# Products of the first two expert units issued unit by unit inside the router stage, and the last token tile scaled and shifted by VectorE

## The chip, the cores and the metric

The kernel runs on one core of a Trainium2 chip. Its time is the device time of one execution in microseconds (us), and the lower of two is the better. Besides TensorE (PE in the rows, its weight loads PEld), VectorE (DVE), ScalarE (ACT), GpSimd (POOL) and SyncE's queue (SP, which issues most transfers) the core has 16 DMA engines, which move data between the device's memory (HBM), SBUF and back.

## The reference, cut to what matters

The model has two layers. Each layer mixes 512 tokens of width 1024 with four branches, normalizes them (layer norm 1, with a gain and a bias), and sends every token to 2 of 32 experts of a hierarchical mixture of experts:

```python
x = _layernorm(alpha * x + mix, ln1_g[l], ln1_b[l])
...
grp_p, grp_idx = lax.top_k(grp_prob, 1)
...
top_p, top_i = lax.top_k(jax.nn.softmax(in_grp, axis=-1), TOP_K)
...
hid = jax.nn.silu(xe @ w_gate[e]) * (xe @ w_up[e])
return hid @ w_down[e]
...
x = _layernorm(alpha * x + ffn, ln2_g[l], ln2_b[l])
```

All matrices are float32. The three matrices of the 32 experts are 3 MB for each expert, some 100 MB in a layer, and every expert's weights are read once in each layer.

## The kernel before, in words

**Stages.** A layer is the mixer (four branches, gates, output projection), then the router stage at the end of the function `mixer`, then the experts in `moe`, then `combine`. The code from the router stage to the experts stands under a manual schedule: every engine gets its instructions in the order in which they are written.

**Router stage.** The four tiles `r[0]` to `r[3]` hold 128 tokens x 1024 each. For each tile the stage adds the residual, takes the statistics, transposes the tile, multiplies it with the router's matrix, and chooses two experts for each token (`R.choose`: maxima, and comparisons whose results are `oo` and `lt`, then `ob`). Tiles 0 to 2 are chosen together, tile 3 later. `R.count` and `R.totals` count with small products how many tokens went to each expert before this one. `R.slots` works out from the counts which token goes to which of 1024 slots; its result `toki` starts the gathers, which fetch the rows of the tokens from `x1_dram`. `R.plan` gives on VectorE the order of the experts by load and writes it into registers that SP reads for the addresses of expert weights.

**Tile 3.** Tiles 0 to 2 are multiplied with the gain (`lng`) and shifted by the bias (`lnb`) on GpSimd in `affine` (L994, L995) and written to `x1_dram` from GpSimd's queue. Tile 3 is scaled on ScalarE (`raw_affine`) and then goes through the same `affine`.

**Units.** Experts 0 to 3 (`LEAD`) are taken in fixed pairs: unit 0 is experts 0 and 1, unit 1 is experts 2 and 3. Their tokens are not gathered: `one_hot(t)` makes a matrix `lone` of 0 and 1 (128 tokens x 4 experts x 64 places), and `lead(t)` multiplies it with `r[t]`. In the kernel before, `lead` takes the four experts in one product of 256 columns, summed over the four tiles in four PSUM banks. In `moe`, `lead_window(u)` copies a unit's columns to SBUF (`xw`), and `gemm(u, c)`, for c from 0 to 3, multiplies them with gate and up weights (L1457; I call these gate products). `hidden(u)`, `hidden_t(u)` and `down(u)` follow with the activation, a transpose and the products with the down weights (L1495). `R.left_over()` and `R.rows()` work out where results are written: a chain between TensorE (L1319 to L1322), VectorE (L1325 to L1358) and TensorE again (L1360). `turned(j)` transposes the j-th gathered tile into `xs` (L1539), from which all later units take their tokens (`window`).

**Weights.** All expert weights pass through `est`, a stream of 1 MB buffers in a ring: 7 `er0`, 2 `raw`, 2 `er2`, then 2 `er1`. I number the transfers of a layer. Transfers 1 to 8 are the gate and up weights of units 0 and 1, 9 to 12 their down weights. Transfer 13 is the first whose address comes from a register. Transfers 14 to 21 go into the buffers of 1 to 8, so each waits until the gate products that read this buffer are done, and 22 goes into the buffer of transfer 9, which `down(0)` reads. All of them are issued in order from SP's queue. The limit on their number is 11 within the router stage, and 22 until the last `turned`:

```python
est.limit = 2 * (ER + MR) + ER_M + ER2
...
turned(7)
ring.cycle += [(R.ep, "er2")] * 2
est.bufs += 2
est.limit = 1 << 30
```

Of the kernel before, what the change touches and what calls it, by code (L numbers as in the profile page):

```python
# [10 lines left out]
F32 = mybir.dt.float32  # L11
# [13 lines left out]
D = 1024  # L25
# [79 lines left out]
def mixer_moe_kernel(ctx: ExitStack, tc: tile.TileContext, a, out, dbg=None):  # L105
# [63 lines left out]
    def ps_mm():  # L169
        return pbank("mm", 3)  # L170

    def ps_s():
        return pbank("s", 2)
# [10 lines left out]
    class Ring:  # L184
# [5 lines left out]
        def more(self, pl, tag, n):  # L190
            self.cycle += [(pl, tag)] * n
            self.bufs[tag] = self.bufs.get(tag, 0) + n
# [126 lines left out]
    def mixer(l, wpool_, wts, raws, xpool, xh, xl, par, ready):  # L319
# [716 lines left out]
        def raw_affine(t):  # L1036
            m = mv[t]
            act(r[t], r[t], AF.Identity, scale=m[:, 2:3], bias=m[:, 3:4])
            affine(t)

        def one_hot(t):

            m = small.tile([128, LEAD, 1], F32, name="lm", bufs=2)
            DVE.scalar_tensor_tensor(m[:, :, 0], R.rank(t), 1.0, R.ob[:, 0, t, :LEAD], op0=OP.add, op1=OP.mult)
            ones[t] = R.ep.tile([128, LEAD, HALF], F32, name="lone", bufs=2)
# [3 lines left out]
        def lead(t, k0=0, k1=KD):  # L1049
            if t + k0 == 0:  # L1050
                R.lead.extend((ps_s(), ps_s(), ps_mm(), ps_mm()))
            for k in range(k0, k1):
                PE.matmul(R.lead[k // 2][:, k % 2 * 256:k % 2 * 256 + 256], r[t][:, k * 128:(k + 1) * 128],
                          ones[t].rearrange("p e j -> p (e j)"), start=t + k % 2 == 0, stop=t == 3, skip_group_check=True)

        ones = {}
# [45 lines left out]
        est = Stream(ep, "er", ER + MR + ER_M + ER2 + 1, 2048)  # L1102
# [19 lines left out]
        raw_affine(3)  # L1122
# [7 lines left out]
        lead(0, 0, 4)  # L1130
# [16 lines left out]
        return R, toki, manual, epool, ring, est, gs  # L1147
# [4 lines left out]
    class routing:  # L1152
# [60 lines left out]
        def slots(self, rp, scratch, beside):  # L1213
# [26 lines left out]
            rone = self.ep.tile([128, 2, 4, 128], BF, name="rone", bufs=1)  # L1240
            pt_ = ps_y()
            for q in range(2):
                for t in range(4):
                    DVE.tensor_scalar(rone[:, q, t], io, low[:, q, t:t + 1], 0.0, op0=OP.add, op1=OP.is_equal)
                    for w in range(2):
                        PE.matmul(pt_[:, :8], rone[:, q, t], hval[:, q, t, w], start=q + t + w == 0,
                                  stop=q + t + w == 5)
# [82 lines left out]
        def rows(self):  # L1330
# [24 lines left out]
            one = T("rone2", [8, 128], BF)  # L1355
            p = ps_t()
            for j in range(8):
                DVE.tensor_scalar(one[:, j], bfc[:, 4], low[:, j:j + 1], 0.0, op0=OP.add, op1=OP.is_equal)  # L1358
                for w in range(2):
                    PE.matmul(p[:, :n], one[:, j], hv[:, w, j], start=j + w == 0, stop=j + w == 8)  # L1360
# [20 lines left out]
    def moe(l, R, toki, manual, epool, ring, est, gs):  # L1381
# [4 lines left out]
        ring.more(er2, "er1", ER2)  # L1386
# [3 lines left out]
        st = {}  # L1390
# [40 lines left out]

        def lead_window(u):
            xw = xa.tile([128, KD, CAP], F32, name="xw", tag="xw", bufs=2)
            for b, p in enumerate(R.lead):
                (DVE.tensor_copy if b % 2 else ACT.copy)(xw[:, 2 * b:2 * b + 2], p.rearrange("p (k n) -> p k n", k=2)[
                    :, :, u * CAP:(u + 1) * CAP])
            st[u] = dict(X=xw)
# [105 lines left out]

        est.limit = 2 * (ER + MR) + ER_M + ER2
        est.bufs = ER + MR + ER_M + ER2 - 1
# [21 lines left out]
        gemm(1, 2)  # L1567
        gemm(1, 3)
# [259 lines left out]
```

## Time and profile before

| what | value |
|---|---|
| time, median of 3 runs | 1587.07 us (1584.9 to 1587.2) |
| the profiled execution | 1588.08 us, of which the span from the first to the last instruction is 1586.3 us |
| busy: PE, DVE, ACT, POOL | 92%, 45%, 36%, 9% of the span |
| granted TensorE clock, mean over the span | 0.972 of full speed |
| transfers | 324.59 MB, mean 205 GB/s |

The profile is of one execution. Times in it count from the start of the span. A granted clock of 1.00 is 2.4 GHz, 0.50 is 1.2 GHz. A row of busy time gives the stretch, its length, the busy time (and instructions) of PE, PEld, DVE, ACT and POOL, then the granted clock, the mean busy share of the DMA engines, and GB/s. A row of a timeline gives start, length, engine, line, what is written and read, shapes and count; the trace counts two instructions for each float32 product, so that x16 in the program's order below is x32 there. The mixer of layer 0 ends at about 493 us, its router stage at about 523 us, its experts at about 760 us; layer 1 has the same stages 787.7 us later, from about 1281 us on.

### The profile page before, as it was taken

The page shows a single profiled execution, that of the slowest core. Times are in us where ns is not written, and L with a number is a line of the kernel's source. Part 1 is how long each engine was busy: PE and PEld are TensorE (multiplying, and loading weights), DVE is VectorE, ACT ScalarE, POOL GpSimd, SP SyncE. Part 2 cuts the span into 40 slices and gives each one's busy share as a digit, 9 for nine tenths or more (in the row PEclk, how much of TensorE's full clock was granted, in tenths as well). Part 3 has the DMA queues.
Part 4 walks back from the last instruction along what each step waited for, and adds up shares of the span by engine and source line. Part 5 has one row for each costly group of instructions (what it writes and reads, how often), then busy time and mean ns, then how long its engine had stood idle before and what let it go on. Part 6 is the DMA issues. An engine that isn't in the chain of part 4 may idle for free. (4 is left out here: it accounts for less than half of the span.)

```text
span 1586.3 us, 17845 instructions
## 1 busy us (share of the span) xinstructions
PE 1463.2 (92%) x6552; PEld 936.0 (59%) x6552; DVE 720.3 (45%) x1382; ACT 564.4 (36%) x1001; POOL 142.8 (9%) x121
## 2 busy tenths in 40 slices
PE   7999999999998999988299999999999989999980
PEld 6766787788887533322197666767888864333320
DVE  7558875434456411110365578864444554111005
ACT  6666435333323211111256654353333223111113
POOL 0000000121006100000000000001210151000000
PEclk9999999999998999999699999999999989999995
DMA  5111122122247999999621121211132579999994
GB/s 212 69 67 67 54 93 83 50 100 93 95 193 293 366 406 423 422 421 418 274 87 54 54 100 54 99 68 67 67 121 86 230 282 381 407 423 421 421 397 169
DMA packets 54042, 324.59 MB, mean 205 GB/s; under 512 B 8640, under 2 KB 9280, under 8 KB 21952
## 3 DMA queue, kind: packets, MB, share of 16 engines
q1 hardware_dynamic: 44880, 299.54, 47.7%
q0 software_dynamic: 9072, 23.89, 4.0%
q8 instruction: 52, 0.85, 0.2%
q14 instruction: 38, 0.31, 0.1%
HBM read 306.62 MB, written 27.26 MB: 210 GB/s over the span
## 5 line engine op out<-in xcount | busy, mean ns | idle before, releaser
L149 PE MATMUL ps_mm<-xh,wh 128*128 128x512 f32 (+1 forms) x768 | 309.1, 403 | 8.7 <-ACT xh L128 8.1
L150 PE MATMUL ps_mm<-xl,wh 128*128 128x512 f32 (+1 forms) x768 | 303.4, 395 | 0.0
L151 PE MATMUL ps_mm<-xh,wl 128*128 128x512 f32 (+1 forms) x768 | 302.4, 394 | 0.0
L1457 PE MATMUL ps_mm<-er,xw 128*64 128x512 f32 (+1 forms) x1024 | 284.9, 598 | 11.2 <-DMA er<-in_w_gu_dram 7.9
L162 DVE TENSOR_TENSOR wl<-raw,wh 128x1280 fp32r<-128x1280 f32 (+2 forms) x116 | 169.7, 1468 | 146.1 <-ACT wh L128 145.8
L1457 PEld LDWEIGHTS ps_mm<-er,xw 128*64 128x64 f32 (+1 forms) x1024 | 88.7, 143 | 175.4 <-issue 143.3
L128 ACT ACTIVATE wh<-raw 128x1280 fp32r<-128x1280 f32 (+2 forms) x116 | 135.2, 1169 | 140.0 <-PE ps_mm L150 99.9
L149 PEld LDWEIGHTS ps_mm<-xh,wh 128*128 128x128 f32 (+1 forms) x768 | 144.1, 188 | 50.6 <-issue 10.1
L151 PEld LDWEIGHTS ps_mm<-xh,wl 128*128 128x128 f32 (+1 forms) x768 | 143.8, 187 | 34.0 <-issue 3.1
L1495 PE MATMUL ps_s<-er,ht 128*64 128x512 f32 (+1 forms) x512 | 147.1, 612 | 17.7 <-DMA er<-in_w_dn_dram 10.7
L150 PEld LDWEIGHTS ps_mm<-xl,wh 128*128 128x128 f32 (+1 forms) x768 | 144.2, 188 | 31.3 <-issue 2.0
L1465 DVE TENSOR_TENSOR sg<-sg,ps_mm 128x256 f32<-128x256 f32 x36 | 15.1, 420 | 253.2 <-ACT sg L128 253.2
L1495 PEld LDWEIGHTS ps_s<-er,ht 128*64 128x64 f32 (+1 forms) x512 | 44.8, 146 | 109.8 <-issue 79.0
L418 POOL TENSOR_TENSOR macc<-macc,sg 128x512 f32<-128x512 f32 x32 | 43.0, 1344 | 697.5 <-PE ps_mm L150 498.9
L128 ACT ACTIVATE sg<-ps_mm,par 128x512 f32<-128x512 f32 x64 | 44.1, 689 | 139.0 <-PE ps_mm L151 139.0
L708 DVE SCALAR_TENSOR_TENSOR cacc<-cvh,par,cacc 128x512 f32<-128x512 f32 x120 | 89.6, 747 | 1.7
L1479 DVE COPY ob<-ps_s 128x512 f32<-128x512 f32 x36 | 24.9, 692 | 132.9 <-PE ps_s L1495 132.9
L417 DVE SCALAR_TENSOR_TENSOR sg<-sg,ps_p 128x512 f32<-128x512 f32 x48 | 33.0, 688 | 105.3 <-PE ps_p L151 97.9
L1484 POOL DMA_INDIRECT ys_dram<-ob,rowi x36 | 35.2, 978 | 407.1 <-DVE xw L1445 301.8
L128 ACT ACTIVATE ht<-ps_t 128x256 f32<-128x256 f32 x36 | 13.8, 383 | 158.3 <-PE ps_t L1472 158.3
L128 ACT ACTIVATE sg<-ps_mm 128x256 f32<-128x256 f32 x36 | 13.8, 383 | 134.7 <-PE ps_mm L1457 134.7
L149 PE MATMUL ps_p<-yh,wh 128*128 128x512 f32 x128 | 51.2, 400 | 0.0
(405 smaller groups left out, 2027.7 us busy)
## 6 DMA issues: line engine op xcount, KB each, us to landing
er<-in_w_gu_dram SPq DMA_DIRECT2D x128, 1024.0 KB, 20.4
er<-in_w_dn_dram SPq DMA_DIRECT2D x64, 1024.0 KB, 21.1
raw<-in_wg_dram SPq DMA_DIRECT2D x32, 1280.0 KB, 5.5
raw<-in_wz_dram SPq DMA_DIRECT2D x12, 1024.0 KB, 4.8
raw<-in_w_o_dram SPq DMA_DIRECT2D x8, 1024.0 KB, 4.8
y<-ys_dram SPq DMA_DIRECT2D x8, 1024.0 KB, 6.6
x_dram<-r POOLq DMA_DIRECT2D x8, 512.0 KB, 8.1
x<-x_dram SPq DMA_DIRECT2D x4, 1024.0 KB, 14.6
```

What stands on the lines that cost most here:

```text
L128: inst = ACT.activation(out_, in_, func, **kw)
L149: PE.matmul(o, x.h, y.h, start=start, stop=False)
L150: PE.matmul(o, x.h, y.l, start=False, stop=False)
L151: PE.matmul(o, x.l, y.h, start=False, stop=stop)
L162: DVE.tensor_tensor(l, src, h, op=OP.subtract)
L417: DVE.scalar_tensor_tensor(sg, sg, 1.0, p2, op0=OP.add, op1=OP.mult)
L418: (DVE if n == 2 else POOL).tensor_tensor(macc[:, d], macc[:, d], sg, op=OP.add)
L708: DVE.scalar_tensor_tensor(cacc[c], cvh[c][:, j:j + S], w, cacc[c], op0=OP.mult, op1=OP.add)
L1457: PE.matmul(s_["p"][h], s_["X"][:, k, h], w[:, k % 4], start=k == 0, stop=k == KD - 1, skip_group_check=True)
L1479: DVE.tensor_copy(ob[:, 512:], p)
L1484: POOL.indirect_dma_start(out=ys_dram[:, :], out_offset=bass.IndirectOffsetOnAxis(ap=idx, axis=0), in_=ob, in_offset=None, bounds_check=SL ...
L1495: PE.matmul(p[h], s_["ht"][:, c, h], w[:, c, hf * 512:(hf + 1) * 512], start=c == 0, stop=c == 1, skip_group_check=True)
```

## The change

In the router stage the products with `lone` are issued for each unit by itself, with 128 columns in place of 256, into two PSUM banks for each unit. Unit 0's products with all four tiles, its copies and its gate products now stand in the router stage, around `R.slots` and `R.plan`; behind them come the products, copies and gate products of unit 1. `moe` then begins with both units' gate products issued. `lone` has four buffers in place of two. Tile 3's gain and bias are applied by VectorE in two instructions between the one-hot matrices of tiles 2 and 3, and its store to `x1_dram` goes out on SP's queue, ahead of transfer 12. The matrices `rone` and `rone2` of the small products get four rotating buffers for the eight pieces. `ring.now` inserts at the ring's present place, which is here the end of the ring, where `more` put it.

```diff
+        def now(self, pl, tag, n):
+            self.cycle[self.at:self.at] = [(pl, tag)] * n
             self.bufs[tag] = self.bufs.get(tag, 0) + n
...
-            DVE.scalar_tensor_tensor(m[:, 3:4], m[:, 0:1], -1.0, m[:, 2:3], op0=OP.mult, op1=OP.mult)
...
         def raw_affine(t):
             m = mv[t]
-            act(r[t], r[t], AF.Identity, scale=m[:, 2:3], bias=m[:, 3:4])
-            affine(t)
+            DVE.scalar_tensor_tensor(r[t], r[t], m[:, 0:1], lng, op0=OP.subtract, op1=OP.mult)
+            DVE.scalar_tensor_tensor(r[t], r[t], m[:, 2:3], lnb, op0=OP.mult, op1=OP.add)
+            SP.dma_start(x1_dram[t * 128:(t + 1) * 128], r[t])
...
+        def lead(u, t):
+
+            if t == 0:
+                pu[u] = [ps_mm(), ps_mm()] if u else [ps_s(), ps_s()]
+            for k in range(KD):
+                PE.matmul(pu[u][k // 4][:, k % 4 * 128:k % 4 * 128 + 128], r[t][:, k * 128:(k + 1) * 128],
+                          ones[t][:, 2 * u:2 * u + 2].rearrange("p e j -> p (e j)"), start=t + k % 4 == 0, stop=t == 3,
+                          skip_group_check=True)
+
+        def lead_window(u):
+            xw = rp.tile([128, D], F32, name="xw", tag="lng" if u else "lnb").rearrange("p (k n) -> p k n", k=KD)
+            for hf in range(2):
+                (DVE.tensor_copy if u and hf else ACT.copy)(xw[:, 4 * hf:4 * hf + 4],
+                                                            pu[u][hf].rearrange("p (k n) -> p k n", k=4))
+            first[u] = dict(X=xw)
...
-        raw_affine(3)
         logits(2)
...
         one_hot(0)
-        lead(0, 0, 4)
+        lead(0, 0)
         raw_logits(3)
         R.choose(3)
         R.count(3)
         R.totals()
         one_hot(1)
-        toki = R.slots(rp, lng, lambda: lead(0, 4, KD))
+        lead(0, 1)
+        one_hot(2)
+        lead(0, 2)
+        raw_affine(3)
+        one_hot(3)
+        toki = R.slots(rp, xt.pop(2).rearrange("p k n -> p (k n)"), lambda: lead(0, 3))
+        est.bufs = ER + MR + ER_M - 1
+        lead_window(0)
+        lead_gemm(0, 0)
+        lead_gemm(0, 1)
         R.kp = ep
         R.weigh()
-        lead(1)
         R.plan()
-        one_hot(2)
-        lead(2)
-        one_hot(3)
-        lead(3)
+        lead_gemm(0, 2)
+        lead_gemm(0, 3)
+        for t in range(4):
+            lead(1, t)
+        lead_window(1)
+        for c in range(4):
+            lead_gemm(1, c)
...
-        est.bufs = ER + MR + ER_M + ER2 - 1
+        est.fill()
         for j in range(6):
             gather(j)
         POOL.memset(xs[:, :, SLOTS:], 0.0)
-        lead_window(0)
-        gemm(0, 0)
-        gemm(0, 1)
-        lead_window(1)
         R.weigh_exp()
-        est.fill()
-        gemm(0, 2)
-        gemm(0, 3)
         R.left_over()
         hidden(0)
-        gemm(1, 0)
-        gemm(1, 1)
         hidden_t(0)
         R.rows()
         turned(0)
         gather(6)
         turned(1)
         gather(7)
-        gemm(1, 2)
-        gemm(1, 3)
         hidden(1)
```

The first place is VectorE's queue in layer 0, from the choice for tile 3 to the first steps of `R.slots`, before. `lm` and `lone` are the two instructions of `one_hot`.

```order
L1191 TENSOR_TENSOR ob_3475<-lt_3474 128x32
L1044 SCALAR_TENSOR_TENSOR lm_3885<-ps_p_3837,ob_3475 128x4
L1046 TENSOR_TENSOR lone_3887<-bfc_103,lm_3885 128x256
L1226 TENSOR_TENSOR lng_3490<-oo_3473,ps_p_3837 128x256
L1228 TENSOR_REDUCE slot_3899<-lng_3490 128x8
```

The same place after the change.

```order
L1227 TENSOR_TENSOR ob_3475<-lt_3474 128x32
L1048 SCALAR_TENSOR_TENSOR lm_3882<-ps_p_3832,ob_3475 128x4
L1050 TENSOR_TENSOR lone_3884<-bfc_103,lm_3882 128x256
L1048 SCALAR_TENSOR_TENSOR lm_3894<-ps_p_3832,ob_3475 128x4
L1050 TENSOR_TENSOR lone_3896<-bfc_103,lm_3894 128x256
L1041 SCALAR_TENSOR_TENSOR r_3484<-r_3484,mv_3792,lng_3490 128x1024
L1042 SCALAR_TENSOR_TENSOR r_3484<-r_3484,mv_3792,lnb_3491 128x1024
L1048 SCALAR_TENSOR_TENSOR lm_3909<-ps_p_3832,ob_3475 128x4
L1050 TENSOR_TENSOR lone_3911<-bfc_103,lm_3909 128x256
L1262 TENSOR_TENSOR xt_3712<-oo_3473,ps_p_3832 128x256
L1264 TENSOR_REDUCE slot_3927<-xt_3712 128x8
```

Two more one-hot matrices and the two instructions over tile 3 now stand ahead of `R.slots`.

The second place is TensorE's queue from the last products with `lone` to the transpose of unit 0's hidden tile (the rows with `sg`), before. Rows that end in 64x512 are gate products, those on `sel`, `one_c` and `dg` are `R.left_over`'s, those on `perm` are `R.plan`'s.

```order
L1053 MATMUL ps_s<-lone,r 128x256 x4
L1053 MATMUL ps_mm<-lone,r 128x256 x4
L1457 MATMUL ps_mm<-er,xw 64x512 x16
L1319 MATMUL ps_t<-sel,plan 1x16
L1320 MATMUL ps_t<-sel,plan 1x16
L1321 MATMUL ps_t<-one_c,plan 1x1
L1322 MATMUL ps_t<-dg,ones_n 128x96
L1457 MATMUL ps_mm<-er,xw 64x512 x8
L1472 MATMUL ps_t<-cst,sg 128x128 x2
```

The same place after the change, from the first gate products on.

```order
L1078 MATMUL ps_mm<-er,xw 64x512 x8
L1328 MATMUL ps_t<-plan,cst 32x1
L1329 MATMUL ps_t<-perm,plan 1x32
L1330 MATMUL ps_t<-perm,plan 1x32
L1078 MATMUL ps_mm<-er,xw 64x512 x8
L1058 MATMUL ps_mm<-lone,r 128x128 x32
L1078 MATMUL ps_mm<-er,xw 64x512 x16
L1355 MATMUL ps_t<-sel,plan 1x16
L1356 MATMUL ps_t<-sel,plan 1x16
L1357 MATMUL ps_t<-one_c,plan 1x1
L1358 MATMUL ps_t<-dg,ones_n 128x96
L1500 MATMUL ps_t<-cst,sg 128x128 x2
```

All 32 gate products now stand ahead of `R.left_over`'s four products, and none between these and what follows the last row, in both kernels: the products of `R.rows` (L1360 before, L1396 after) and the transposes of gathered tiles. Before, 8 gate products stood ahead of the last row, and 8 more between the transposes of gathered tiles 1 and 2.

## Rows read from the trace of the kernel before

**Rows 1.** Busy time by stage, layer 0; last columns: granted clock, DMA share, GB/s.

```profile
505.00:527.00 22.00, 20.54 (x114) 15.06 (x114) 12.24 (x72) 4.69 (x10) 7.53 (x9) 0.95 0.56 196
527.00:560.00 33.00, 30.23 (x179) 14.89 (x176) 14.23 (x43) 8.46 (x16) 3.00 (x3) 1.00 0.97 386
560.00:640.00 80.00, 79.50 (x318) 27.12 (x319) 9.96 (x21) 13.03 (x28) 6.83 (x7) 1.00 1.01 416
640.00:755.00 115.00, 104.86 (x368) 33.43 (x364) 11.58 (x24) 15.09 (x32) 7.79 (x8) 1.00 1.01 420
```

**Rows 2.** Timeline of SP's queue (start, duration): transfers 14, 20 and 22.

```profile
527.17 0.34 SPq L225 DMA_DIRECT2D er<-in_w_gu_dram  x1
...
542.67 0.33 SPq L225 DMA_DIRECT2D er<-in_w_gu_dram  x1
...
549.66 0.33 SPq L225 DMA_DIRECT2D er<-in_w_gu_dram  x1
```

**Rows 3.** Timeline of TensorE, layer 0 (start, duration, idle time before in brackets).

```profile
482.07 1.87 PE L988 MATMUL ps_t<-wr,xt 128*128 128x36 f32 x16
...
504.07 3.46 PE L1053 MATMUL ps_s<-lone,r 128*128 128x256 f32 x8 [0.80 <-DVE lone L1046]
...
511.24 1.97 PE L1053 MATMUL ps_s<-lone,r 128*128 128x256 f32 x8
...
523.49 7.09 PE L1457 MATMUL ps_mm<-er,xw 128*64 128x512 f32 x32
530.51 0.20 PE L1319 MATMUL ps_t<-sel,plan 32*1 32x16 f32 x2
...
535.92 1.35 PE L1360 MATMUL ps_t<-rhv,rone 128*128 128x34 bf16 x16 [0.79 <-DVE rone L1358]
537.12 1.07 PE L1539 MATMUL ps_s<-cst,g 128*128 128x128 f32 x8
...
545.98 3.65 PE L1495 MATMUL ps_s<-er,ht 128*64 128x512 f32 x16 [0.35 <-DVE xs L1541]
...
558.01 2.41 PE L1457 MATMUL ps_mm<-er,xw 128*128 128x512 f32 x5 [1.43 <-ACT xw L1445]
```

**Rows 4.** Timeline of VectorE, layer 0, in the router stage.

```profile
497.66 2.12 DVE L1188 TENSOR_TENSOR oo<-cst,ei 128x192 bf16<-128x192 f32 x1
499.70 2.49 DVE L1188 TENSOR_TENSOR lt<-cst,ei 128x192 bf16<-128x192 f32 x1
...
505.84 0.23 DVE L1188 TENSOR_TENSOR oo<-cst,ei 128x64 bf16<-128x64 f32 x1
...
508.21 0.41 DVE L1226 TENSOR_TENSOR lng<-oo,ps_p 128x256 f32<-128x256 bf16 x1
...
515.73 0.14 DVE L1044 SCALAR_TENSOR_TENSOR lm<-ps_p,ob 128x4 f32<-128x4 f32 x1
...
516.25 0.15 DVE L1044 SCALAR_TENSOR_TENSOR lm<-ps_p,ob 128x4 f32<-128x4 f32 x1
```

**Rows 5.** Timeline of GpSimd in the same stretch.

```profile
497.22 2.34 POOL L994 TENSOR_TENSOR r<-r,lng 128x1024 f32<-128x1024 f32 x1 [3.21 <-ACT r L128]
499.64 2.34 POOL L995 TENSOR_TENSOR r<-r,lnb 128x1024 f32<-128x1024 f32 x1
```

**Rows 6.** Groups of instructions on VectorE (busy us, mean ns).

```profile
L1665 DVE SCALAR_TENSOR_TENSOR x<-x,mv,ln 128x1024 f32<-128x1024 f32 x8 | 10.1, 1267 | 0.0
```

**Rows 7.** Busy time in windows of 1 us, columns as in group 1.

```profile
497.00:498.00 1.00, 1.00 (x7) 1.00 (x6) 0.96 (x9) 0.13 (x1) 0.78 (x1) 0.50 1.04 356
...
507.00:508.00 1.00, 0.96 (x9) 0.54 (x8) 0.29 (x2) 0.00 (x0) 0.00 (x0) 0.95 0.00 0
557.00:558.00 1.00, 0.00 (x0) 0.00 (x0) 0.62 (x2) 0.87 (x3) 0.00 (x0) 1.00 0.95 393
...
1295.00:1296.00 1.00, 0.80 (x8) 0.50 (x6) 0.58 (x3) 0.16 (x1) 0.00 (x0) 0.71 0.00 0
```

**Rows 8.** Timeline of TensorE, layer 1: the first products with the one-hot matrix.

```profile
1291.43 3.75 PE L1053 MATMUL ps_s<-lone,r 128*128 128x256 f32 x8 [0.81 <-DVE lone L1046]
```

More of the change, by code (lines that the diff above doesn't have):

```diff
@@ L1044, in one_hot, with lead_gemm @@
             DVE.scalar_tensor_tensor(m[:, :, 0], R.rank(t), 1.0, R.ob[:, 0, t, :LEAD], op0=OP.add, op1=OP.mult)
-            ones[t] = R.ep.tile([128, LEAD, HALF], F32, name="lone", bufs=2)
+            ones[t] = R.ep.tile([128, LEAD, HALF], F32, name="lone", bufs=4)
             DVE.tensor_tensor(ones[t], bc(bfc[:, 4, None, 1:HALF + 1], [128, LEAD, HALF]), bc(m, [128, LEAD, HALF]),
                               op=OP.is_equal)
[L1049 to L1054, printed above, removed]
+        def lead(u, t):
[11 more added lines that the diff above has]
+            first[u] = dict(X=xw)
+        def lead_gemm(u, c):
+            s_ = first[u]
+            if c == 0:
+                s_["p"] = ps_mm()
+            if c % 2 == 0:
+                s_["w"] = [est.get().rearrange("p (k n) -> p k n", n=512) for j in range(2)]
+            for k in (2 * c, 2 * c + 1):
+                for j, w in enumerate(s_["w"]):
+                    h = slice(j * HALF, (j + 1) * HALF)
+                    PE.matmul(s_["p"][h], s_["X"][:, k, h], w[:, k % 4], start=k == 0, stop=k == KD - 1,
+                              skip_group_check=True)
+        pu, first = {}, {}
         ones = {}
@@ L1135, in mixer @@
         one_hot(1)
-        toki = R.slots(rp, lng, lambda: lead(0, 4, KD))
+        lead(0, 1)
[8 more added lines that the diff above has]
+        lead_gemm(0, 1)
         R.kp = ep
         R.weigh()
-        lead(1)
         R.plan()
-        one_hot(2)
-        lead(2)
-        one_hot(3)
-        lead(3)
+        lead_gemm(0, 2)
[5 more added lines that the diff above has]
+            lead_gemm(1, c)
         for p in (rpool, wpool_):
             close(p)
-        return R, toki, manual, epool, ring, est, gs
+        return R, toki, manual, epool, ring, est, gs, first
     def bc(x, shape):
@@ L1243, in slots @@
                 for t in range(4):
-                    DVE.tensor_scalar(rone[:, q, t], io, low[:, q, t:t + 1], 0.0, op0=OP.add, op1=OP.is_equal)
+                    rone = self.ep.tile([128, 128], BF, name="rone", bufs=4)
+                    DVE.tensor_scalar(rone, io, low[:, q, t:t + 1], 0.0, op0=OP.add, op1=OP.is_equal)
                     for w in range(2):
-                        PE.matmul(pt_[:, :8], rone[:, q, t], hval[:, q, t, w], start=q + t + w == 0,
+                        PE.matmul(pt_[:, :8], rone, hval[:, q, t, w], start=q + t + w == 0,
                                   stop=q + t + w == 5)
@@ L1354, in rows @@
             DVE.tensor_scalar(hv[:, 1], hone, cst[:, C_ROW + 8:C_ROW + 9], None, op0=OP.mult)
-            one = T("rone2", [8, 128], BF)
             p = ps_t()
             for j in range(8):
-                DVE.tensor_scalar(one[:, j], bfc[:, 4], low[:, j:j + 1], 0.0, op0=OP.add, op1=OP.is_equal)
+                one = self.kp.tile([128, 128], BF, name="rone2", bufs=4)
+                DVE.tensor_scalar(one, bfc[:, 4], low[:, j:j + 1], 0.0, op0=OP.add, op1=OP.is_equal)
                 for w in range(2):
-                    PE.matmul(p[:, :n], one[:, j], hv[:, w, j], start=j + w == 0, stop=j + w == 8)
+                    PE.matmul(p[:, :n], one, hv[:, w, j], start=j + w == 0, stop=j + w == 8)
             rowi = self.kp.tile([128, n], I32, name="rowi")
@@ L1379, in weigh_exp, with moe @@
             table.update(users=[])
-    def moe(l, R, toki, manual, epool, ring, est, gs):
+    def moe(l, R, toki, manual, epool, ring, est, gs, st):
         regs = R.regs
@@ L1385, in moe @@
         ering, er2 = pool("est2")
-        ring.more(er2, "er1", ER2)
+        ring.now(er2, "er1", ER2)
         apool, xa = pool("xa")
@@ L1389, in moe @@
         R.kp = xb
-        st = {}
         nxt = []
@@ L1430, in halves @@
             return [slice(0, CAP)] if wide(u) else [slice(0, HALF), slice(HALF, CAP)]
[L1432 to L1437, printed above, removed]
         def window(u):
```

5 lines of the change are left out of this document (3 added, 2 removed).

## The prediction

> **What bounds the kernel now.** I read the page first: TensorE is busy for most of the span, and the transfers move at full rate in two long stretches, the experts of the two layers. The stages of layer 0 [rows 1] say which of the two sets the end there. From 560 to 640 us TensorE is busy for 79.5 of 80 us, and the DMA engines are full as well. From 640 to 755 us TensorE idles 10 of 115 us and the DMA engines none: TensorE has used up its lead and waits for weights. So the experts end when the weights have come. At 420 GB/s a transfer of 1 MB takes 2.5 us, and a gather of half that size 1.25 us. What can still be won lies where the DMA engines idle: 44% of 22 us (505 to 527) and 3% of 33 us (527 to 560), 9.7 + 1.0 = 10.7 us in a layer.
>
> They idle because every buffer is full. The queue of SP shows who frees them [rows 2]: transfer 14 goes out at 527.17, when the first half of unit 0's gate products is done (these start at 523.49 [rows 3] and take 7.0 us in all). Transfer 22 goes out at 549.66, when `down(0)` ends: 545.98 + 3.65 = 549.63 [rows 3]. Transfers 14 to 21 and the two last gathers are 8 x 2.5 + 2 x 1.25 = 22.5 us of work from 527.17 on, which is over at 549.7. So the DMA engines run dry just where `down(0)` lets them go on. **From there on the layer is one stream of weights, and its end moves with the end of `down(0)`**, or with the transfers ahead of it if these are later.
>
> **The change part by part, in layer 0.** Layer 1 repeats these rows 787.7 us later, and I count it the same.
>
> (a) VectorE's comparisons `oo` and `lt` of tiles 0 to 2 take 2.12 and 2.49 us [rows 4], while GpSimd works on tile 3 from 497.22 to 501.98 [rows 5]. Each of them ends 0.2 us after one of GpSimd's instructions. With a third of the columns and GpSimd at rest the same comparison takes 0.23 us [rows 4]. The change takes tile 3 from GpSimd. I price the two at 0.35 us each, between 0.23 and three times that: 3.9 us gained. The bounds are 3.2 and 4.1 us, and nothing, if the length is their own (a rival below).
>
> (b) TensorE's first products with the one-hot matrix run at half clock: it has been 0.50 since 497 [rows 7], before the idle time that (a) shortens, so I expect it again. 16 instructions of 128 columns stand for 8 of 256, which take 3.46 us from 504.07 [rows 3]. No change; the 3.9 us reach the choice for tile 3.
>
> (c) VectorE gets more to do ahead of `R.slots`: two more one-hot matrices at 0.52 us (515.73 to 516.25, [rows 4]), and two instructions over tile 3 at 1.27 us by the nearest shape [rows 6], 3.6 us in all. `R.slots` starts at 508.21 - 3.9 + 3.6 = 507.9 [rows 4]. So what (a) gave, (c) takes, and the token list and the plan come within 0.3 us of where they were. Tile 3's store leaves SP's queue at about 507.4, ahead of transfer 12. Both go out while the DMA engines idle. The gathered tiles are first read at 537.12 [rows 3], and transfer 12 is read only by `down(1)`, which covers them; without that cover the half megabyte would cost its 1.25 us and transfer 12 its 2.5 us.
>
> (d) TensorE is through with the token list's products at about 511.2 in both; then it had the rest of the one-hot products (511.24 to 523.49, [rows 3]). Now: gate products of unit 0, 7.0 us, with some 0.3 us of waiting for the plan and 0.35 us for its three products in the middle, until 518.9. Then unit 1's one-hot products, 64 instructions in the trace's count: from below by the 36-column products at 482.07, 1.87 / 16 = 0.117 us each with the last one's tail in it, from above by half of a 256-column one at 511.24, 1.97 / 16 = 0.123. I take 0.11 without the tail, 7.1 us, until 526.0 (6.8 to 7.9). A copy to SBUF shows 0.1 us, since its first half is done while the last products run. Gate products of unit 1, 7.0 us, until 533.1.
>
> (e) `R.left_over`'s first product stood at 530.51 and now stands at 533.1. From there to the first transpose of a gathered tile at 537.12 [rows 3] are 6.6 us: a chain from TensorE to VectorE and back. Before, half of unit 1's gate products lay in it and covered 3.6 us of it. Now all of them stand ahead of it, and only two transposes are left to cover it. So this is what is late next: the transposes start at 533.1 + 6.6 = 539.7, 2.6 us later than before.
>
> (f) From 537.12 to `down(0)` at 545.98 are 8.9 us, of which 3.55 us were the other half of unit 1's gate products (7.09 / 2, [rows 3]). That leaves 5.3 us, and `down(0)` starts at 545.0, **1.0 us earlier** than before. With an uncertainty of 1 us from (a), (c) and (d).
>
> (g) The clock. From 533.7 to 539.7 TensorE has next to nothing: two transposes and 16 small products of 34 columns. A gap of 1.43 us ahead of 558.01 [rows 3] left the clock at 1.00 [rows 7]. The stretch of waiting and small products ahead of 504.07 ended with it at 0.50. The new stretch is four times the gap that cost nothing, so I expect the clock to fall. It came back at 507.05 (a mean of 0.95 in that microsecond), 3.0 us after the products at 504.07 had begun, and in layer 1 at 1295.6 (0.71), 4.2 us after those at 1291.43 [rows 7, 8]. At half rate for 3.0 to 4.2 us, TensorE loses 1.5 to 2.1 us; I take 1.8. `down(0)` then starts at 546.8, **0.8 us later** than before. If the clock holds, nothing is lost.
>
> The Trainium skill, in "TensorE: Matmul & The Clock Gate", section "HAM oscillation — how this bites in real kernels", holds that a burst of products behind a wait starts at half rate again. By it every layer pays (g), and the sum is 1.6 us more; by the row at 557 alone, where a wait cost nothing, it is 2.0 us less. The trace agrees with the page ahead of 504.07 and not at 557.
>
> (h) `ring.now` puts the last two buffers where they were, and the four rotating `rone` buffers are emptied by TensorE at least as fast as VectorE fills them: nothing.
>
> **Sum.** 2 x (-1.0 + 1.8) = +1.6 us. The profiled execution took 1588.08 us, 1.8 us more than its span and 1.0 us above the median; it would take 1589.7, and the median 1587.07 becomes **1588.7 us**.
>
> **The rivals.** A difference of less than 0.2%, 3.2 us, is about what a measurement of this kernel can't tell from none.
>
> *The early buffers decide (faster).* Gate products now free buffers at about 514.8, 519, 529.6 and 533.1, where transfer 14 went at 527.17 and transfer 20 at 542.67 [rows 2]. From 511.5, when the gathers start, transfers 13 to 21 and eight gathers are 9 x 2.5 + 8 x 1.25 = 32.5 us of work: done at 544.0 in place of 549.7. If the layer's end followed, it would come 5.7 us earlier, and the kernel would take 1587.07 - 11.4 = 1575.7 us. For it speaks the idle DMA time [rows 1]. Against it: transfer 22 needs the buffer that `down(0)` reads, and that product would have to end by 544.0; by (f) it ends after 548. Chance 0.10.
>
> *The clock holds.* Then (g) falls away: 1587.07 - 2.0 = 1585.1 us. Chance 0.13.
>
> *Transposes don't bring the clock back.* It fell at 497 with TensorE busy for the whole microsecond [rows 7], in small products. If the transposes of gathered tiles don't raise it either, all 5.3 us of (f) run at half rate, and the first 3 us of `down(0)` too: 5.3 + 1.5 = 6.8 us lost in place of 1.8, and 1587.07 + 2 x 5.8 = 1598.7 us. A half of that is as likely, 1593. It decides from the moment at which the clock in the transposes reads 0.50 to their end. Chance 0.12.
>
> *`oo` and `lt` are slow by themselves.* Then (c) comes on top: all from `R.slots` on is 3.9 us later, 1588.7 + 7.8 = 1596.5 us. Against it speaks the 0.23 us of the smaller form. Chance 0.05.
>
> Other waits that I don't see, all on the slow side: 0.05. The forecast keeps 0.55.
>
> **How the numbers follow.** The forecast by itself spans 1585.5 to 1591.5: (f) to within 1 us and (g) from 1.5 to 2.1 us, in two layers. The range runs from 1583.5, which takes in the case in which the clock holds, to 1594.5, which takes in the milder half of the third rival. Left out are the first rival (0.10), the fourth, and the worse half of the third: 0.2 in all. Faster by over 0.2% are the first rival and a little of the second: 0.13. Slower are the third, the fourth, the unseen waits and the forecast's upper end: 0.27. Within 0.2%: 0.60.
>
> **What would show it.** In the profile after: `oo` and `lt` at 0.3 to 0.4 us each, and `R.slots` at about the same time as before (a, c). Transfer 14 at about 516 and transfer 21 at about 533 us, then the DMA engines idle until `down(0)` ends, at 548.6 to 551 (d, f). TensorE nearly idle for some 5 us between unit 1's gate products and the transposes (e), with the clock at 0.50 behind it (g). DMA share 1.0 from then on, and TensorE waiting for weights near the end of the layer. I am wrong if transfer 22 goes out well ahead of 548 (then the first rival), if `R.slots` starts late, or if the stream of weights isn't what ends the layer.

## The result, and the profile after

The changed kernel takes 1608.88 us (median of 4 runs, 1606.17 to 1609.65); the kernel before, beside it, 1587.13 us. The ratio is 1.0134, with a 95% interval from 1.0116 to 1.0152, so the kernel got slower by 1.3%. The forecast was 1588.7 us within 1583.5 to 1594.5: wrong by 20 us. The profiled execution took 1608.98 us, with a span of 1607.2 us.

I read the stages first. These rows of the changed kernel answer to [rows 1]; one stage ahead of them is added.

```profile
460.00:493.00 33.00, 32.65 (x172) 27.20 (x173) 19.18 (x33) 11.03 (x29) 15.72 (x8) 1.00 0.29 107
...
505.00:527.00 22.00, 21.62 (x170) 16.04 (x169) 9.44 (x45) 2.02 (x4) 0.58 (x2) 1.00 1.01 422
527.00:560.00 33.00, 22.90 (x119) 13.09 (x117) 12.43 (x45) 7.75 (x15) 9.00 (x9) 0.74 1.01 417
560.00:640.00 80.00, 78.36 (x322) 28.51 (x320) 13.28 (x30) 14.68 (x30) 6.89 (x7) 1.00 1.00 405
640.00:755.00 115.00, 106.29 (x381) 34.63 (x378) 12.27 (x25) 15.64 (x33) 8.79 (x9) 1.00 1.01 421
```

From 505 to 527 us the DMA engines are full where they idled 44% of the time, and yet TensorE is busy for only 23 of the 33 us that follow, at a clock of 0.74. The reason stands in the added row: from 460 to 493 us the DMA engines moved 107 GB/s. The same stretch of the kernel before, which I had not looked at, had 389.

```profile
460.00:493.00 33.00, 32.60 (x172) 27.15 (x172) 19.04 (x33) 10.81 (x29) 15.91 (x8) 1.00 0.95 389
```

SP's queue says what is missing there. In the kernel before, transfers 1 to 8 go out from 460.68 us on (start, duration, line, what is written, count); the last row stands near the end of the layer's experts and serves as a mark.

```profile
460.68 8.90 SPq L225 DMA_DIRECT2D er<-in_w_gu_dram  x8
471.75 22.53 SPq L225 DMA_DIRECT2D er<-in_w_dn_dram  x4
...
743.26 0.39 SPq L1518 DMA_DIRECT2D x<-x_dram  x1
```

The same queue of the changed kernel:

```profile
493.42 4.40 SPq L229 DMA_DIRECT2D er<-in_w_gu_dram  x8
498.95 7.73 SPq L229 DMA_DIRECT2D er<-in_w_dn_dram  x3
508.88 0.33 SPq L1043 DMA_DIRECT2D x_dram<-r  x1
511.31 0.33 SPq L229 DMA_DIRECT2D er<-in_w_dn_dram  x1
517.30 13.91 SPq L229 DMA_DIRECT2D er<-in_w_gu_dram  x6
...
560.54 1.25 SPq L229 DMA_DIRECT2D er<-in_w_gu_dram  x2
...
753.74 0.39 SPq L1546 DMA_DIRECT2D x<-x_dram  x1
```

Transfer 1 goes out **32.7 us later**, and with it all that stand behind it in SP's order; tile 3's store has eleven of them ahead of it. The mark at the end is 10.5 us late; two layers make the 20.9 us by which the span has grown (layer 1's transfer 1 goes out at 1291.02, right behind the end of its mixer too). What SP waits for is in its waits (who for whom, us in total, times, longest): a product of L151, the last of the mixer's output projection.

```profile
SPq L229 <- PE ps_mm L151: 32.4, 1, 32.4
```

Why a weight buffer should wait for the output projection is not in the trace but in the places in SBUF that the built program gave to the tiles. Bytes per partition, before and after:

```
                               before              after
ml (read by L151)       149472 .. 165856    149472 .. 165856
buffer of transfer 1    166016 .. 174208    164992 .. 173184
```

The buffers of the stream lie in the pool `est`, whose upper end is fixed, so that it grows downward. Two more buffers `lone` make it 2 KB wider, the four small `rone` 1 KB narrower. So the buffer of transfer 1, which had 160 free bytes below it, now reaches 864 bytes into `ml`, which is read until the output projection ends, and the transfer must wait until nothing reads these bytes any more. No line of the diff says so.

The store that leaves at 508.88 lands 18.6 us later (DMA issues: KB each, median us to landing; the changed kernel first, from 500 to 535 us, then the kernel before, from 495 to 530 us).

```profile
x_dram<-r SPq DMA_DIRECT2D x1, 512.0 KB, 18.6
```

```profile
x_dram<-r POOLq DMA_DIRECT2D x1, 512.0 KB, 4.5
```

The gathers read what it writes. GpSimd starts the first at 528.32, where the prediction had 511.5 (the row names VectorE as the releaser, but what VectorE gives the gather is `toki`, done at 512.5).

```profile
509.75 0.58 POOL L1275 TENSOR_TENSOR hval<-hone,cst 128x64 bf16<-128x64 f32 x2 [15.56 <-ACT prs L1288]
528.32 1.08 POOL L1559 DMA_INDIRECT g<-x_dram,toki  x1 [17.98 <-DVE sel L1341]
```

These rows of TensorE answer to [rows 3]: the first half of unit 0's gate products, unit 1's gate products, `left_over`, `rows`, transposes of gathered tiles, `down(0)`, and the next unit's gate products.

```profile
512.22 3.65 PE L1078 MATMUL ps_mm<-er,xw 128*64 128x512 f32 x16
...
527.20 7.09 PE L1078 MATMUL ps_mm<-er,xw 128*64 128x512 f32 x32
534.22 0.20 PE L1355 MATMUL ps_t<-sel,plan 32*1 32x16 f32 x2
...
540.36 1.38 PE L1396 MATMUL ps_t<-rhv,rone 128*128 128x34 bf16 x16 [2.89 <-DVE rone L1394]
541.58 1.95 PE L1567 MATMUL ps_s<-cst,g 128*128 128x128 f32 x8
...
549.63 1.09 PE L1567 MATMUL ps_y<-cst,g 128*128 128x128 f32 x4 [3.64 <-DMA g<-x_dram,toki]
...
553.39 1.94 PE L1567 MATMUL ps_s<-cst,g 128*128 128x128 f32 x8 [1.39 <-DMA g<-x_dram,toki]
555.26 5.25 PE L1523 MATMUL ps_s<-er,ht 128*64 128x512 f32 x16
...
568.88 1.55 PE L1485 MATMUL ps_mm<-er,xw 128*128 128x512 f32 x3 [1.44 <-ACT xw L1473]
```

Until 534 us all is within 1.1 us of the prediction. Then TensorE waits twice for gathers, 5.0 us in all, and much of the rest runs at half clock (8 transposes in 1.95 in place of 1.07 us). `down(0)` begins at 555.26, 8.5 us after its forecast.

VectorE in the router stage, answering to [rows 4]:

```profile
497.60 0.36 DVE L1224 TENSOR_TENSOR oo<-cst,ei 128x192 bf16<-128x192 f32 x1
497.88 0.35 DVE L1224 TENSOR_TENSOR lt<-cst,ei 128x192 bf16<-128x192 f32 x1
...
505.14 1.28 DVE L1041 SCALAR_TENSOR_TENSOR r<-r,mv,lng 128x1024 f32<-128x1024 f32 x1
506.45 1.29 DVE L1042 SCALAR_TENSOR_TENSOR r<-r,mv,lnb 128x1024 f32<-128x1024 f32 x1
...
508.19 0.42 DVE L1262 TENSOR_TENSOR xt<-oo,ps_p 128x256 f32<-128x256 bf16 x1
...
509.52 0.87 DVE L1280 TENSOR_SCALAR rone<-bfc,low 128x128 bf16<-128x128 bf16 x4
511.29 0.74 DVE L1280 TENSOR_SCALAR rone<-bfc,low 128x128 bf16<-128x128 bf16 x4 [0.91 <-PE ps_y L1282]
```

`oo` and `lt` take 0.71 us together where they took 4.61, as forecast. New is the wait of 0.91 us between the fourth and the fifth `rone`.

### The profile page after: what moved, and what is told of

Its sections match the earlier page's. It is cut to its first block, busy times and chain, and to the rows that moved or that the text cites. A ratio compares the mean times of both kernels' runs of the same rounds, so it can differ in the third digit from the quotient of the medians.

```text
span 1607.2 us, 18107 instructions
## 1 busy us (share of the span) xinstructions
PE 1474.9 (92%) x6680; PEld 949.6 (59%) x6680; DVE 716.9 (45%) x1378; ACT 563.1 (35%) x997; POOL 132.5 (8%) x115
## 5 line engine op out<-in xcount | busy, mean ns | idle before, releaser
L151 PE MATMUL ps_mm<-xh,wl 128*128 128x512 f32 (+1 forms) x768 | 302.4, 394 | 0.0
L1485 PE MATMUL ps_mm<-er,xw 128*64 128x512 f32 (+1 forms) x896 | 256.5, 599 | 10.3 <-DMA er<-in_w_gu_dram 6.9
L1485 PEld LDWEIGHTS ps_mm<-er,xw 128*64 128x64 f32 (+1 forms) x896 | 80.1, 144 | 158.8 <-issue 128.6
L151 PEld LDWEIGHTS ps_mm<-xh,wl 128*128 128x128 f32 (+1 forms) x768 | 143.8, 187 | 34.0 <-issue 3.1
L1509 ACT ACTIVATE ob<-ps_s 128x512 f32<-128x512 f32 x36 | 21.5, 597 | 85.3 <-PE ps_s L1523 85.3
```

The costliest lines, as they stand in the source:

```text
L151: PE.matmul(o, x.l, y.h, start=False, stop=stop)
L1485: PE.matmul(s_["p"][h], s_["X"][:, k, h], w[:, k % 4], start=k == 0, stop=k == KD - 1, skip_group_check=True)
```

## The experiments

Theory: the overlap of transfer 1's buffer with `ml` starts the stream 33 us late; the stream and the store behind it cost the 21 us. Rivals: a store on SP's queue is late by itself; the low clock and the bare chain of `left_over` and `rows` cost it.

| kernel | median us | ratio to before, 95% |
|---|---|---|
| changed | 1608.88 | 1.0134 [1.0116, 1.0152] |
| one_buffer_out | 1591.83 | 1.0024 [1.0013, 1.0034] |
| room_192 | 1601.87 | 1.0084 [1.0068, 1.0099] |
| room_128 | 1587.56 | 1.0000 [0.9989, 1.0011] |
| store_by_gpsimd | 1601.98 | 1.0090 [1.0075, 1.0105] |
| rone_whole | 1589.79 | 1.0004 [0.9994, 1.0015] |
| clock_held | 1586.62 | 0.9984 [0.9975, 0.9994] |
| tile3_as_before | 1600.44 | 1.0071 [1.0056, 1.0086] |
| tile3_alone | 1586.11 | 0.9982 [0.9973, 0.9991] |
| chain_early | 1575.93 | 0.9912 [0.9897, 0.9928] |
| chain_early_room_192 | 1601.76 | 1.0076 [1.0059, 1.0093] |

The runs came in three groups: one_buffer_out to store_by_gpsimd; rone_whole to tile3_as_before, and chain_early; tile3_alone and chain_early_room_192. The kernel before ran beside each group, at 1588.2, 1589.0 and 1589.7 us; the ratios go by these, so kernels of different groups are better compared by their ratios than by their medians. The last products of L988 (L992 after the change), where the router stage begins, stand at 491.3 to 494.2 us in the traces. Where I say by how much a place in one kernel is earlier or later than in another, it is counted from these products.

**one_buffer_out: the overlap taken away.**

```diff
-            ones[t] = R.ep.tile([128, LEAD, HALF], F32, name="lone", bufs=4)
+            ones[t] = (rp.tile([128, LEAD, HALF], F32, name="lone", bufs=1) if t > 2 else
+                       R.ep.tile([128, LEAD, HALF], F32, name="lone", bufs=3))
```

> The changed kernel with one of the four lone buffers (1 KB per partition) in the pool rpool, so that the pool est is as wide as before the change. Theory: in the changed kernel est is 1 KB wider, the buffer of transfer 1 reaches 864 bytes into ml, which the output projection reads until 493.1 us, and so all expert transfers of a layer start at 493.4 in place of 460.7. Then here transfer 1 goes out at about 460.8, tile 3's store lands less than 6 us after it goes out, the first gather goes out at about 513, down(0) starts at 545 to 548, and the time is 1584 to 1592 us. First rival: a store on SP's queue lands late because it stands behind weights, whenever these started: it lands 15 us or more after it goes out, the first gather stays behind 524, and the time above 1600. Second rival: the low clock and the bare chain of left_over and rows cost the 20 us: gathers early, time above 1600.

Of 1.34% above the kernel before, 0.24% is left. SP's queue and TensorE's:

```profile
460.12 8.63 SPq L229 DMA_DIRECT2D er<-in_w_gu_dram  x8
...
507.47 0.33 SPq L1043 DMA_DIRECT2D x_dram<-r  x1
```

```profile
533.94 0.20 PE L1356 MATMUL ps_t<-sel,plan 32*1 32x16 f32 x2
...
540.56 1.95 PE L1568 MATMUL ps_s<-cst,g 128*128 128x128 f32 x8
...
547.59 3.65 PE L1524 MATMUL ps_s<-er,ht 128*64 128x512 f32 x16 [0.34 <-DVE xs L1570]
...
559.61 10.72 PE L1486 MATMUL ps_mm<-er,xw 128*128 128x512 f32 x32 [1.44 <-ACT xw L1474]
```

The store lands 2.9 us after it goes out (DMA issues from 500 to 530 us), and the first gather goes out at 513.05.

```profile
x_dram<-r SPq DMA_DIRECT2D x1, 512.0 KB, 2.9
```

The theory holds, and as causes of the 21 us both rivals fall: the same store, the same low clock and the same bare chain are here, and the kernel is 4 us above the kernel before. These 4 us are what all gains and losses of the change leave together; clock and chain by themselves cost more, as clock_held and chain_early show.

**room_192 and room_128: the overlap brought into the kernel before, and nearly.** In both, `rone2` gets its four rotating buffers, which makes the room in `xb`, and `rone` is padded:

```diff
-            rone = self.ep.tile([128, 2, 4, 128], BF, name="rone", bufs=1)
+            rone = self.ep.tile([128, 2, 4, 140], BF, name="rone", bufs=1)[:, :, :, :128]
```

(136 in place of 140 in room_128.)

> The kernel before with the pool est 192 bytes per partition wider (rone padded) and rone2 in four rotating buffers, which makes the room in xb. 160 bytes lay free between ml and the buffer of transfer 1; now they overlap by 32 bytes. Theory: transfer 1 goes out at about 493.3 in place of 460.7, though nothing else is changed; 12 transfers, the store and six gathers are done at about 532 in place of 526, transfers 14 to 21 come up to 6 us later in each layer, and the time is 1593 to 1602 us. Rival: the place of the buffers is harmless, and the changed kernel is slow by its new order: 1587 within 3 us.

> The same as room_192 with 128 bytes in place of 192, so that 32 bytes stay free. Theory: transfer 1 goes out at 460.7, and the time is that of the kernel before, 1587 within 3 us. If it is slower as room_192 is, the shift itself or rone2 is the cause and not the overlap.

128 bytes more change nothing, 192 bytes cost 13 us. SP's queue of room_192, then of room_128:

```profile
494.29 4.59 SPq L225 DMA_DIRECT2D er<-in_w_gu_dram  x8
```

```profile
461.33 8.76 SPq L225 DMA_DIRECT2D er<-in_w_gu_dram  x8
```

So the new order of the products is not needed for a loss of this kind. In room_192 tile 3's store goes out from GpSimd's queue, as before, and lands after 8.1 us; `down(0)` is 0.4 us late and the mark 7.2 us. Here the late weights alone cost the time.

**store_by_gpsimd: what the late store adds.**

```diff
-            SP.dma_start(x1_dram[t * 128:(t + 1) * 128], r[t])
+            POOL.dma_start(x1_dram[t * 128:(t + 1) * 128], r[t])
```

> The changed kernel with tile 3's store issued from GpSimd's queue in place of SP's; the place of the buffers stays. Theory: transfer 1 stays at 493.4, but the store no longer stands behind eleven transfers on one queue: it lands 5 to 9 us after it goes out, as the stores of before did beside transfers, the first gather goes out at 514 to 518, and half or more of the 21.7 us comes back: 1590 to 1600 us. If the gathers' lateness is all of the loss, 1587 to 1590. Rival: the DMA engines are full until 535 in any case and the store lands as late: 1605 or more.

Transfer 1 still goes out at 493.21. The store lands after 8.1 us, the first gather goes out at 516.75, and `down(0)` begins at 547.68, as in one_buffer_out.

```profile
x_dram<-r POOLq DMA_DIRECT2D x1, 512.0 KB, 8.1
```

A third of the loss comes back (7 of 21 us); the least that I expected was half. The other 10 us above one_buffer_out stay, though `down(0)` is back in its place: a stream that starts 33 us late stays late.

**The ledger.** Sums of length times GB/s over ten windows from 460 to 755 us, beside the mark at the end of layer 0's experts (both as each trace counts them):

| kernel | MB moved, 460 to 755 us | mark, us |
|---|---|---|
| before | 115.6 | 743.26 |
| changed | 111.3 | 753.74 |
| store_by_gpsimd | 112.6 | 750.07 |
| one_buffer_out | 114.8 | 744.78 |
| chain_early | 117.6 | 738.26 |

Each MB missing puts the mark 2.3 to 2.5 us later (1.9 us for the 0.8 MB of one_buffer_out), and 1 MB at 420 GB/s is 2.4 us. So in these five kernels the mark follows the time for which the DMA engines idled ahead of it. This is bookkeeping: it says where time was lost, and the runs above say why. The late start took 282 GB/s x 33 us = 9.3 MB; the idle time behind 493 us gave about half of it back. The changed kernel loses 1.3 MB more than store_by_gpsimd, nearly all from 560 to 600 us (388 against 421 GB/s). Over half of that is lost in the first 10 us, where the engines run dry (215 GB/s until 562) while transfer 22, which had to wait for `down(0)`, goes out at 560.54.

**rone_whole: the rotation of `rone` undone.** `rone` is one tile of eight pieces again; for its space, two `lone` lie in a tile `xt` that is free by then.

```diff
-                    rone = self.ep.tile([128, 128], BF, name="rone", bufs=4)
-                    DVE.tensor_scalar(rone, io, low[:, q, t:t + 1], 0.0, op0=OP.add, op1=OP.is_equal)
+                    DVE.tensor_scalar(rone[:, q, t], io, low[:, q, t:t + 1], 0.0, op0=OP.add, op1=OP.is_equal)
```

> The changed kernel, with rone again in one tile of eight pieces, and two of the four lone buffers inside a tile xt that is free by then, so that est is as wide as before the change (as in one_buffer_out). In one_buffer_out VectorE waits 0.91 us in the middle of the eight rone pieces for TensorE to empty the first four. Theory: the list's products, the gate products of unit 0 and down(0) come 0.9 us earlier in each layer, so the time is 1.8 us below that of one_buffer_out: 1590.0, between 1588.5 and 1591. Rival (my prediction's step h): the rotation costs nothing, the same as one_buffer_out within 1 us.

2.0 us less by the medians, 3.2 us by the ratios. The eight pieces now take 1.52 us without a wait:

```profile
510.32 1.52 DVE L1283 TENSOR_SCALAR rone<-bfc,low 128x128 bf16<-128x128 bf16 x8
```

Unit 0's gate products come 0.7 us earlier than in one_buffer_out, and `down(0)` 1.4 us, more than the 0.9 us of the theory: the clock also comes back sooner in the transposes (a mean of 0.88 from 543 to 544 us, where one_buffer_out, whose trace runs 1 us ahead, still has 0.50). Why it does is open.

**clock_held: the waits of TensorE filled.**

```diff
+            fill(4)
...
         hidden_t(0)
+        fill(13)
         R.rows()
...
+    def fill(n):
+        p = ps_y()
+        for j in range(n):
+            PE.matmul(p, ones_b, bfc[:, 0:4].rearrange("p a b -> p (a b)"), start=True, stop=True)
```

> one_buffer_out with 4 products of 512 columns (bf16, constants, into an unused PSUM bank; results not read) behind left_over's products and 13 more behind unit 0's transposes, which fill the 1.25 and 3.07 us in which TensorE waits for VectorE. Theory (step g): the waiting is what lowers the clock; with it filled the first transposes of gathered tiles take 1.1 in place of 1.95 us, down(0) starts 1.5 to 2.1 us earlier in each layer, and the time is 3 to 4 us below one_buffer_out: 1588. Rivals: the clock falls all the same, or the filling delays the products of rows: no gain, or up to 1 us per layer more.

1586.62 us: 5.2 us less than one_buffer_out by the medians, 6.3 us by the ratios, where 3 to 4 us were expected.

```profile
536.48 2.97 PE L1192 MATMUL ps_y<-bfc,ones_b 128*128 128x512 bf16 x13
539.71 1.35 PE L1403 MATMUL ps_t<-rhv,rone 128*128 128x34 bf16 x16 [0.26 <-DVE rone L1401]
540.91 1.07 PE L1574 MATMUL ps_s<-cst,g 128*128 128x128 f32 x8
...
546.07 3.65 PE L1530 MATMUL ps_s<-er,ht 128*64 128x512 f32 x16 [0.37 <-DVE xs L1576]
```

The transposes run at full clock from the first, and `down(0)` comes 1.84 us earlier than in one_buffer_out (547.59 less 546.07, and 0.32 us by which the router stage begins later). Two layers make 3.7 us. The mark comes 2.6 us earlier, and two layers of that make 5.1 us; why it gains more than `down(0)` does is open.

**tile3_as_before and tile3_alone: tile 3 by itself.** The first is one_buffer_out with `raw_affine` as before the change, at its old place:

```diff
         raw_columns(3, 1)
+        raw_affine(3)
         logits(2)
...
-        raw_affine(3)
         one_hot(3)
```

The second is the kernel before with the changed `raw_affine`, ahead of `R.slots`:

```diff
-        raw_affine(3)
         logits(2)
...
         one_hot(1)
+        raw_affine(3)
```

> one_buffer_out with tile 3 scaled by ScalarE and GpSimd and stored from GpSimd's queue, as before the change. Steps (a) and (c) of the prediction: oo and lt of tiles 0 to 2 take 2.1 to 2.5 us each again (+3.9), VectorE is rid of the two instructions over tile 3 (-2.6), so the slots, the list and down(0) come 1.3 us later in each layer: 2.6 us above one_buffer_out, 1594.4. If VectorE's share is covered by TensorE's one-hot products, the whole 3.9 us per layer: 1599. Rival: the choice for tile 3 is hidden and nothing changes, 1592 within 1.

> The kernel before with tile 3's part of the change alone: gain and bias by VectorE ahead of the slots, store on SP's queue; the products stay four experts wide and est stays as wide as it was. Steps (a) and (c): oo and lt 3.9 us shorter, two instructions of 1.3 us more ahead of the slots, so the slots and all behind them come 1.3 us earlier in each layer: 2.6 us below before, 1584.5. If instead TensorE's products cover VectorE's two instructions, as tile3_as_before showed for the new order (8.6 us in all), 1580. The store has no weights ahead of it, lands in under 5 us and delays nothing. Rival: a store on SP's queue delays the gathers here too, 1587 or more.

Alone, the move gives 2.9 us by the ratios, as the sum of steps (a) and (c) has it (2.6). In the new order it gives 8.6 us by the medians (7.5 by the ratios), not the 2.6 of that sum but the case named behind it, in which TensorE covers VectorE's share: there `oo` and `lt`, at 2.11 and 2.49 us again, put off unit 0's next one-hot products by 4.2 us and the slots by only 1.6, and the list's products come 4.2 us later: TensorE, not VectorE's work ahead of the slots, sets the list's time. The store on SP's queue lands 2.9 us after it goes out in tile3_alone: with no weights ahead of it, it delays nothing.

**chain_early: `left_over` and `rows` under the one-hot products.**

```diff
         lead_gemm(0, 3)
+        R.kp = rp
+        R.big = xt[3].rearrange("p k n -> p (k n)")
+        R.left_over()
         for t in range(4):
             lead(1, t)
+        R.rows()
         lead_window(1)
...
-        R.left_over()
         hidden(0)
         hidden_t(0)
-        R.rows()
```

Their larger tiles lie in `R.big`, `rone2` in `rone`, and `est` stays as wide as before the change.

> rone_whole with left_over and rows moved into the router stage: left_over's four products behind unit 0's gate products, rows' products behind unit 1's one-hot products, VectorE's part of both while TensorE multiplies with lone. Theory (steps d to f): then nothing stands between unit 1's gate products and the transposes of gathered tiles but unit 0's two transposes; these begin at about 535, 5 us earlier than in rone_whole, at full clock, so down(0) starts at about 540. The layer's end moves with it until the transfers ahead of transfer 22 (done at about 544 by the first rival's sum) are the last to come: 5 to 6 us less in each layer than before, 1575 to 1579 us. Rival: the layer's end does not follow down(0) any more, since the DMA engines are full in any case: 1586 to 1590.

1575.93 us, the fastest of all: 0.9912 of the kernel before. TensorE, SP's queue, and the stage from 527 to 545 us:

```profile
533.62 1.04 PE L1574 MATMUL ps_s<-cst,g 128*128 128x128 f32 x8
...
538.74 3.65 PE L1530 MATMUL ps_s<-er,ht 128*64 128x512 f32 x16 [0.38 <-DVE xs L1576]
```

```profile
542.42 1.25 SPq L229 DMA_DIRECT2D er<-in_w_gu_dram  x2
```

```profile
527.00:545.00 18.00, 17.62 (x106) 9.20 (x104) 5.53 (x10) 6.96 (x15) 3.95 (x4) 1.00 1.02 420
```

Transfer 22 goes out the moment `down(0)` ends (538.74 + 3.65 = 542.39), and the DMA engines are full all the while.

The time lies in the expected range, but not for the expected reason alone. The span is 11.9 us shorter than before. From the beginning of the router stage to the mark it is 4.1 us in layer 0, and from there to the end of the span 4.7 us in layer 1, where 5 to 6 were expected of each. The other 3 us lie in the two mixers, in which this edit changes no line; layer 1's mixer is 2.0 us shorter in chain_early_room_192 as well. Why is open, so up to 3 us of the gain may not belong to the moved chain.

**chain_early_room_192: the overlap in the fastest kernel**, by the padding of room_192.

> chain_early with est 192 bytes wider by the same padding of rone, so that the buffer of transfer 1 overlaps ml by 32 bytes. In chain_early the DMA engines idle little behind 512 us, so there is less idle time left that could take in the late start than in the kernel before. Theory: transfers 1 to 11 go out from 493.3 on; by 755 us 117.6 MB were moved in chain_early and 112.8 MB can be here (10.5 MB until 512, then 421 GB/s), 4.8 MB less or 11.5 us in each layer: 1576 + 23 = 1599, up to 1606 if the gathers' lateness holds up down(0) as well. Rival: the late start costs what it cost in room_192, 13 us: 1589.

It costs 25.8 us here, more than the 13 us in the kernel before. From 460 to 493 us the DMA engines move 94 GB/s, and little idle time is left behind that could take it in:

```profile
460.00:493.00 33.00, 32.48 (x184) 27.76 (x182) 19.75 (x34) 9.87 (x28) 16.64 (x9) 1.00 0.25 94
```

One thing more differs from room_192: tile 3's store stands on SP's queue here. It lands after 18.7 us, TensorE waits for gathers, `down(0)` begins only at 552.85, and from 545 to 600 us 0.9 MB less is moved than in chain_early. By 755 us 5.8 MB are missing in all, so by the ledger about a sixth of the cost hangs on the queue and the rest on the late start; no run parts the two.

## Why the prediction was wrong

**The steps that failed** are (h) and, through it, (c). (h) says: "`ring.now` puts the last two buffers where they were, and the four rotating `rone` buffers are emptied by TensorE at least as fast as VectorE fills them: nothing." It costs the buffers `lone` and `rone` in time and nowhere in space, though the diff makes four buffers out of two in a full memory. A term "where do the stream's buffers lie now, and who reads there" was missing. What the runs showed in its place: transfer 1's buffer reached 864 bytes into `ml`, and the stream began at 493.42 in place of 460.68.

With that, (c) lost its ground: "Tile 3's store leaves SP's queue at about 507.4, ahead of transfer 12. Both go out while the DMA engines idle. The gathered tiles are first read at 537.12 [rows 3], and transfer 12 is read only by `down(1)`, which covers them". It took from the kernel before that transfers 1 to 11 are done by 507 us. They had begun only at 493.42, and the DMA engines were full from 505 us on. The price that (c) named for a store without cover, 1.25 and 2.5 us, was far too low too: the store lands 18.6 us after it goes out. With the stream on time (one_buffer_out) it lands after 2.9 us, and (c) holds.

The size of it, by the ratios: 1.34 - 0.24 = 1.10%, 17 us. Of these 7 us hang on the store's queue (store_by_gpsimd), 10 us on the late stream. The rotation of `rone`, which (h) also put at nothing, is another 0.24 - 0.04 = 0.20%, 3 us: VectorE runs four pieces ahead and then waits 0.91 us for TensorE, which is still at its one-hot products. Together they are the 20 us by which the forecast was wrong.

The Trainium skill, in "DMA: Bandwidth & Descriptors", section "Issuing engines are not separate DMA queues", holds that transfers of different engines run on the same 16 DMA engines and interleave, so that spreading them over issuing engines saves only the time to issue them. Here another issuing engine made 18.6 us into 8.1 with the DMA engines equally full (422 and 419 GB/s from 512 to 527 us), so the measurement differs from the page: which queue the store stood in, and what stood ahead of it there, counted for more than issuing.

**What was right.** Without the overlap and the rotation of `rone` (rone_whole) the ratio is 1.0004 [0.9994, 1.0015]; the forecast, 1588.7 to 1587.07, is 1.0010. In its trace `down(0)` is 0.3 us later than before, forecast 0.8, and the mark is where it was.

- (a) `oo` and `lt`: 0.36 and 0.35 us, forecast 0.35 each.
- (b) The first one-hot products ran at half clock again: in one_buffer_out 16 instructions of 128 columns from 499.87 us in 3.76 us, the next 32 in 3.81.
- (c) VectorE's two instructions, 1.28 and 1.29 us, forecast 1.27; slots at 508.19, forecast 507.9.
- (d) Unit 1's one-hot products took 7.34 us (519.86 to 527.20), forecast 7.1; `left_over` at 534.22, forecast 533.1.
- (e) The bare chain took 6.6 us in one_buffer_out (533.94 to 540.56), as forecast.
- (f, g) From there to `down(0)` 7.0 us (540.56 to 547.59), forecast 5.3 + 1.8. The clock is the cause of the 1.8: with the waits filled it is 5.2 us (540.91 to 546.07). In one_buffer_out it reads 0.50 from the first transposes on, 1.00 from 545 us. The Trainium skill, in "TensorE: Matmul & The Clock Gate", section "HAM oscillation — how this bites in real kernels", has a burst behind a wait start at half rate again; here the traces agree with it (1.95 us for 8 transposes behind the wait, 1.07 us with the wait filled). The prediction held the row at 557 against the page; the wait there, 1.43 us, is shorter than those that the section describes, so that row says nothing against it.
- **The model**, that a layer's end moves with the end of `down(0)`, holds roughly while the stream starts on time: in one_buffer_out `down(0)` is 1.7 us and the mark 1.6 us later than before; in chain_early they are earlier by 6.3 and 4.1 us. The second is near the limit that the prediction named: with the DMA engines full from 527 us on, the transfers ahead of transfer 22 are as late as `down(0)`. In store_by_gpsimd `down(0)` is 1.8 us late and the mark 6.9: there the weights decide.

**The rivals.** The early buffers did not decide: in one_buffer_out they come early too, and transfer 22 still waits for `down(0)`. What that rival lacked, `down(0)` ended by 544.0, is there in chain_early (542.39), whose 1575.93 us lie beside its 1575.7; in part that is luck, since 3 us of the gain lie in the mixers. The transposes brought the clock back where the gathers were there in time (by 545 us in one_buffer_out). `oo` and `lt` were not slow by themselves. What happened stood under "other waits that I don't see", with a chance of 0.05.

## What to carry to other kernels

In a kernel with a full SBUF, a diff that adds a buffer moves others: compare the places of the tiles, and what the first transfer of each stream waits for, before and after, ahead of any sum over instructions. 32 bytes of overlap cost 13 to 26 us here, 32 bytes of room nothing. Where a layer ends when its weights have come, add up the bytes that the DMA engines move by a fixed time; that sum finds the stage in which they idled, however far ahead of the place where TensorE waits. And what a gather needs should not stand behind weights in one queue: here that cost 15.7 us from the store to its landing, and 7 us of the time.

## What was unexpected of the hardware

A store of 512 KB on SP's queue landed 2.9 us after it went out with the DMA engines idle (one_buffer_out, tile3_alone), and 18.6 to 19.5 us after with eleven transfers of 1 MB ahead of it that had begun 15 us earlier. On GpSimd's queue beside the same load it took 8.1 us.
